# Decay of the RWKV-7 state taken out of the transposed keys: an identity product in place of a POOL product, transposes in place of a diagonal product

## The chip, the core and the metric

The kernel runs on one core of one Trainium2 chip, in one launch. The metric is the device time of that core in microseconds (us), as the median of a few executions; lower is better. The core has a matrix engine (TensorE, PE in the profile, with its weight loads as PEld), a vector engine (VectorE, DVE), an activation engine (ScalarE, ACT), a general engine (GpSimd, POOL) and a queue engine (SyncE, SP). Each works through its own instructions in a fixed order, and semaphores hold an instruction back until what it needs is there. Matrix results land in PSUM, in banks of 512 float32 columns; everything else lies in SBUF.

## What is computed

The reference is a trunk of two layers on a sequence of 512 tokens of 1024 features. Layer 0 mixes tokens with a spatial gating MLP, layer 1 with RWKV-7 time mixing; each is followed by a gated feed-forward block with a causal convolution, and an RMS norm stands ahead of each part and at the end. The change lies in the time mixing alone. Its core, per head (16 heads of 64 features), is a recurrence over tokens on a 64 x 64 state:

```python
def step(state, inp):
    r_t, w_t, k_t, v_t, a_t, b_t = inp
    sa = jnp.einsum('bhvk,bhk->bhv', state, a_t)
    state = (state * w_t[:, :, None, :]
             + sa[..., None] * b_t[:, :, None, :]
             + v_t[..., None] * k_t[:, :, None, :])
    y_t = jnp.einsum('bhvk,bhk->bhv', state, r_t)
    return state, y_t
```

Here w is a decay between 0 and 1 for each feature and token, `exp(-exp(...))` of a low-rank projection; a is minus the normalised key, and b the normalised key times a gate. Behind the recurrence come a group norm, a bonus term r·k·v, an output gate and the projection w_o.

## The kernel before

The work runs in phases: sgu, ffn0, rwkv, ffn1, and the final norm. Dense products are made in three passes of a split float32 (lines 283 to 285: high x high, high x low, low x high). Only the rwkv phase matters here, and in it two loops.

The recurrence is done in chunks of C = 64 tokens, NCH = 8 chunks. With the cumulated decay inside a chunk, the products of all its tokens become small matrix products, and a 64 x 64 triangular system per chunk and head is inverted once. Two heads share the 128 partitions: head 0 the lower half, `H[0]`, head 1 the upper half, `H[1]`. A pair p is two heads; there are 8 pairs, four to a group g.

**The pairs loop** (`pairs`, line 914) walks the pairs. For each, `decay` (line 814) is run two pairs ahead. It makes the cumulated log decay `th`: a tanh on ACT (line 824), plus one on DVE (line 827), a scan along the tokens on DVE (line 829). From it come `gt = exp(C1*th)`, the decay from the chunk's start up to each token; `ei = exp(-C1*th)`, its inverse; and `gc` (line 835), the decay over a whole chunk. It also makes the key's norm, with products on PE (lines 841 and 849). `operands` (line 853), one pair ahead, multiplies: `ar` holds key and receptance times the decay, `bk` holds `b * ei` and `k * ei` (lines 871 and 873), and `rr = rr * kp` for the bonus is made on POOL (line 874). `products` (line 878) makes the chunk's inner products on PE (line 892), masks them on DVE (line 896) and stores them in DRAM (`std`). Then it makes the transposed keys `bt` with the decay to the chunk's end. For that, DVE lays out `dg`, a diagonal matrix of `gc` for each chunk (line 885), PE multiplies `bk` by it (line 907: 16 products for a pair), ACT copies the result and a DMA stores it in DRAM (`btd`).

In `invert` (line 941) the triangular systems of a group are inverted; most of that is a long run of DVE operations (lines 966 and 967) and 32 x 32 products (lines 987 and 990).

**The scan** (`scan`, line 1032) runs group 0, then group 1, over the 8 chunks. In each chunk `st` (inner products), `bt` and `vu` are loaded from DRAM. `vu` holds for each head the state in one half of the partitions and v in the other. A chunk has three steps, each ending in a `yield`. Step A: the product with the state and v into the bank `us` (line 1059), its copy `wt` on DVE (line 1061), the receptance's product into the bank `e` (line 1063), and, on POOL, `s0`, the state times `gc` (line 1068, one instruction a head). Step B: the inverse applied (line 1072, into `us`), and the result copied over the state's place in `vu`, head 0 by DVE (line 1073), head 1 by ACT (line 1074). Step C: the update of the state into `us` (line 1079), the new state as `us + s0` on DVE into the next chunk's `vu` (line 1082, one instruction a head), the rest of the output into `e` (line 1084) and its copy `y` on ACT (line 1087). Every second chunk a `finish` (line 1095) is started, a few instructions per step: group norm (square on ACT, sum on DVE line 1103, power on POOL line 336, product on DVE line 1106), transposes on PE (line 1110), gate and bonus.

**The order of the work.** A scheduler lays out each engine's order beforehand. `weave` (line 1215) runs a main generator and, after each of its steps, pulls `rate` steps (a fraction is carried over) of a fill generator: dense products on PE that fill what the main loop leaves. A pulled step may be placed no earlier than the end of the main step `lag` steps back. `RATES` (line 31) holds rate and lag for five places: two in the pairs loop, then scan 0, scan 1, and the last `finish`. In the pairs loop and scan 0 the fill is `projections` (keys and values); in scan 1 it is `project` (w_o), which for a group pulls 16 dense steps of two k-tiles, six products each, and yields empty until that group's outputs are gated. `scan(1)` has 24 steps; group 0 is gated in its fifth. In `value` (line 783) v is stored to DRAM (`vtd`), from which the scan loads it.

A PSUM accumulator with a tag (`aux`, `e`, `us`, `mm`) is one bank, two to a tag.

Of the kernel before, what the change touches and what calls it, by code (L numbers as in the profile page):

```python
# [24 lines left out]
C = 64  # L25
# [2 lines left out]
GN_EPS = 64e-5  # L28
C1 = -0.5 * math.exp(-0.5)

RATES = ((1.9, 2), (1.9, 6, 2.2), (0.8, 2, 2), (0.75, 2), (2, 2))
WB = 4
FIRST0, WAIT, STEPS = 1, 1, (2, 2, 2, 2, 2)
NKEY = 3
# [15 lines left out]
NG = 2 * 16 + 8  # L50


COFF = dict(ident=0, bones=128, center=256, masks=384, smask=512, causal=1024, blk2=1152, one=1154, id2=1155)
NCST = 1219


def constants():
    c = np.zeros((P, NCST), np.float32)
    i = np.arange(P)
    same = (i[:, None] // C) == (i[None, :] // C)  # L60
    c[:, 0:128] = np.eye(P)
    c[:, 128:256] = same
    c[:, 256:384] = np.eye(P) - same / C
    s, t = (i % C)[:, None], np.arange(C)[None, :]
    c[:, 384:448] = s < t
    c[:, 448:512] = s <= t
    c[:, 512:1024] = (np.arange(T) % C != 0)[None, :]
    c[:, 1024:1152] = i[:, None] <= i[None, :]
    c[:, 1152:1154] = (i[:, None] // C) == np.arange(2)[None, :]
    c[:, 1154] = 1.0  # L70
    c[:, 1155:1219] = (i % C)[:, None] == np.arange(C)[None, :]
    return c


# [68 lines left out]
class Emit:  # L143
# [558 lines left out]
    def rwkv_main(self, r, ctx, gain):  # L702
# [10 lines left out]
        def tile_(shape, tag, bufs):  # L713
            return ep.tile(shape, F32, tag=tag, bufs=bufs, name=self.uid(tag))
# [7 lines left out]
        def bc(t, n):  # L722
            return t.unsqueeze(2).to_broadcast([t.shape[0], t.shape[1], n])
# [17 lines left out]
        def projections():  # L741

            load = Ahead([lambda n=n, m=m: self.parts(n, m, m % 3 == 2) for n in PARTS for m in range(KT)])

            def key(m, a):
                while m >= NKEY and m - NKEY not in used:
                    yield
                ks[m] = tmp("key", NKEY, T)
                S.copy(ks[m], a)

            for m in range(KT - 2):
                a = self.acc("mm")
                yield from self.dense_steps(a, load.take(), r.xk)
                yield from key(m, a)
                yield

            ws = [load.take(), load.take(False)]
            accs = [self.acc("mm") for _ in range(2)]
            xv = []
            for k in range(KT):  # L760
                for j in range(2):
                    self.mm3(accs[j], self.wcols(ws[j], k * P, P), r.xk[k], k == 0, k == KT - 1)
                while len(xv) < min(k + 3, KT):
                    xv.append(r.mix(3, len(xv)))
                if k == 4:
                    load.fetch()
                yield
            for j in range(2):
                yield from key(KT - 2 + j, accs[j])
            late = iter(())  # L770
            for m in range(KT):
                a = self.acc("mm")
                for _ in self.dense_steps(a, load.take(), xv):
                    yield
                    next(late, None)
                for _ in late:
                    yield
                v = ip.tile([P, T], F32, tag="v", bufs=1, name=self.uid("v"))
                S.copy(v, a)
                late = value(m, v)  # L780
            yield from late
# [32 lines left out]
        def decay(p, u):  # L814

            k, w = ks[p], slice(p % 2 * P, (p % 2 + 1) * P)
            accs = [self.acc("e") for _ in range(2)]
            for j in range(2):
                nc.tensor.matmul(accs[j], l2[j][:, w], r.lr[j], start=True, stop=False)
            for j in range(2):  # L820
                nc.tensor.matmul(accs[j], l2[2][H[j], w], r.lr[j][H[j]], start=False, stop=True)
            th, u.ta = scratch("sq"), tmp("ta", 2, T)
            for j, x in enumerate((th, u.ta)):
                S.activation(x, accs[j], AF.Tanh, scale=0.5, bias=dq(j, p))
            u.kn = tmp("kn", 2, T)
            S.activation(u.kn, k, AF.Copy, scale=dq(2, p))
            V.tensor_scalar(th, th, 1.0, None, ALU.add)
            yield
            V.tensor_tensor_scan(th, self.c("smask", T), th, 0.0, ALU.mult, ALU.add)
            sq = scratch("sq")  # L830
            S.activation(sq, u.kn, AF.Square)
            u.gt = tile_([P, NCH, C + 1], "gt", 1)
            G.memset(u.gt[:, :, 0:1], 1.0)
            S.activation(u.gt[:, :, 1:], c3(th), AF.Exp, scale=C1)
            S.activation(gc[:, p], c3(th)[:, :, C - 1], AF.Exp, scale=C1)
            u.ei = scratch("rb")
            S.activation(u.ei, th, AF.Exp, scale=-C1)

            q = self.acc("e")
            for b in range(4):  # L840
                nc.tensor.matmul(q[:, 2 * b:2 * b + 2], sq[:, b * P:(b + 1) * P], self.c("blk2", 2), start=True, stop=True)
            n2 = tile_([P, 8], "n2", 2)
            V.tensor_scalar(n2, q[:, 0:8], 1e-24, None, ALU.max)
            V.reciprocal(n2, n2)
            yield
            u.q = self.acc("e")
            for b in range(4):
                for hd in range(2):
                    nc.tensor.matmul(u.q[H[hd], b * P:(b + 1) * P], n2[:, 2 * b + hd:2 * b + hd + 1].to_broadcast([P, C]),
                                     self.c("ident", P), start=True, stop=True)  # L850
            yield

        def operands(p, u):

            g, i = divmod(p, 4)
            k, rr = ks[p], rt[g][:, i, :]
            gt, ei, kn, ta = u.gt, u.ei, u.kn, u.ta
            kp = scratch("ss")
            S.activation(kp, ta, AF.Identity, scale=dq(4, p), bias=dq(5, p))

            ar = u.ar = tile_([P, NCH, 2 * C], "ar", 2)
            V.tensor_tensor(ar[:, :, 0:C], c3(kn), gt[:, :, 0:C], ALU.mult)
            V.tensor_tensor(ar[:, :, C:], c3(rr), gt[:, :, 1:], ALU.mult)
            for hd in range(2):
                o = 2 * P * hd
                nc.sync.dma_start(std[g][:, H[hd], i, o:o + P].rearrange("c p t -> p c t"), ar[H[hd]])

            bk = u.bk = tile_([P, NCH, 3 * C], "bk", 2)
            V.tensor_tensor(kn, kn, u.q, ALU.mult)
            V.scalar_tensor_tensor(ta, ta, 1.0, ei, ALU.add, ALU.mult)  # L870
            V.scalar_tensor_tensor(bk[:, :, 0:C], c3(kn), -0.5, c3(ta), ALU.mult, ALU.mult)
            V.tensor_tensor(kp, kp, k, ALU.mult)
            V.tensor_tensor(bk[:, :, C:P], c3(kp), c3(ei), ALU.mult)
            G.tensor_tensor(rr, rr, kp, ALU.mult)
            used.add(p)
            S.copy(bk[h1, :, P:], bk[h1, :, 0:C])

        def products(p, u):
# [1 line left out]

            g, i = divmod(p, 4)
            ar, bk = u.ar, u.bk

            dg = tile_([P, NCH, C], "dg", 1)
            V.tensor_tensor(dg, self.c("id2", C).unsqueeze(1).to_broadcast([P, NCH, C]), bc(gc[:, p], C), ALU.mult)
            masks = self.c("masks", P)

            for ch in (slice(0, U), slice(U, NCH)):
# [15 lines left out]
            qs = [self.acc(tag).rearrange("p (c t) -> p c t", t=C) for tag in ("aux", "us")]  # L904
            for c in range(NCH):
                for hd in range(2):
                    nc.tensor.matmul(qs[hd][:, c, :], bk[H[hd], c, C * hd:C * hd + P], dg[H[hd], c, :],
                                     start=True, stop=True)
            for hd in range(2):
                S.copy(bt[:, :, hd, :], qs[hd])  # L910
            nc.sync.dma_start(btd[:, :, p].rearrange("c p a t -> p c (a t)"), bt.rearrange("p c a t -> p c (a t)"))
# [120 lines left out]
        def scan(g, late=iter(())):  # L1032
# [3 lines left out]
            for c in range(NCH):  # L1036
# [20 lines left out]

                for i, hd in ih:
                    nc.tensor.matmul(us[H[hd], 0, i, :], ar(i, hd, 0), vu[:, hd, i, :], start=True, stop=True)  # L1059
                wt = tile_([P, 4, C], "wt", 4)  # L1060
                V.tensor_copy(wt, us[:, 0])
                for i, hd in ih:
                    nc.tensor.matmul(e[H[hd], 0, i, :], ar(i, hd, 1), vu[:, hd, i, :],
                                     start=i == 0, stop=False, skip_group_check=True)
                if not last:
                    s0 = tile_([P, 4, C], "wt", 4)
                    for hd in range(2):
                        G.tensor_tensor(s0[H[hd]], vu[H[hd], hd], bc(gc[H[hd], 4 * g:4 * g + 4, c], C), ALU.mult)
                self.step(late)
                yield  # L1070
                for i, hd in ih:
# [4 lines left out]
                yield  # L1076
                if not last:
                    for i, hd in ih:
                        nc.tensor.matmul(us[H[hd], 0, i, :], bt[:, i, hd, :], vu[:, hd, i, :], start=True, stop=True)
                    nvu = chunks[g, c + 1][2]  # L1080
                    for hd in range(2):
                        V.tensor_tensor(nvu[H[hd], hd], us[H[hd], 0], s0[H[hd]], ALU.add)
                for i, hd in ih:
                    nc.tensor.matmul(e[H[hd], 0, i, :], pt(i, hd), vu[H[hd], hd, i, :],
                                     start=False, stop=True, skip_group_check=True)
# [187 lines left out]
```

## Time and profile before

| | us |
|---|---|
| median of 3 runs | 1321.42 |
| lowest and highest | 1318.86 and 1322.74 |
| profiled execution | 1320.36 |
| its span, first to last instruction | 1318.5 |

In the profiled execution, the pairs loop runs from about 594 to 762 us of the span, scan 0 from 773, scan 1 from about 846 to 906; sgu and ffn0 lie ahead, the rest of `project`, ffn1 and the final norm behind. The profile page gives busy time and number of instructions of each engine, and of each group of instructions by line, with what the engine was waiting for just before them. A view of stretches gives the busy time of each engine in a stretch of time, with the clock that was granted to TensorE (1.00 is full speed). The chain of work is followed back from the last instruction: at each step to whatever released it, or to the instruction before it on its engine. A timeline row has start and length in us, engine, line, what is written from what, the shape and, in brackets, idle time of the engine just before it and who ended it. A float32 product on PE leaves two records (two weight loads and two matmuls), and a matmul's record is longer than the distance from one to the next, because matmuls are pipelined.

### The profile page before, as it was taken

What the parts mean: (1) busy time and instruction counts of PE and PEld (TensorE: products, weight loads), DVE (VectorE), ACT (ScalarE), POOL (GpSimd) and SP (SyncE); (2) the same over time, 40 slices, a digit from 0 to 9 for tenths busy, and PEclk for the clock granted to TensorE, in tenths of its full rate; (3) what the DMA queues carried; (4) which work ended last, traced back from release to release, by engine and by line L of the source; (5) the groups of instructions that cost most, each with busy time, mean ns of one, the idle gap of its engine ahead of it and who ended that gap; (6) DMA issues with size and microseconds to landing.
All of it is one profiled execution on the core that took longest, in us unless ns stands there. A gap on an engine that the chain in (4) does not pass through costs nothing.

```text
span 1318.5 us, 19535 instructions
## 1 busy us (share of the span) xinstructions
PE 1271.9 (96%) x7618; PEld 1027.9 (78%) x7618; DVE 848.0 (64%) x1363; ACT 626.4 (48%) x1064; POOL 141.8 (11%) x152
## 2 busy tenths in 40 slices
PE   8999999999999999999999978898999999999996
PEld 6778888888888888786777757676888888888886
DVE  5565488887775434865879575666687777772223
ACT  5544455555554333565667545333554445442221
POOL 3100200000000100311121011332300000000001
PEclk9999999999999999999999887999999999999998
DMA  7232345555556743245887695971333332233332
GB/s 261 85 112 80 112 148 173 166 168 174 170 174 213 219 141 109 88 126 165 246 254 215 181 237 134 214 190 43 96 96 97 96 96 96 96 92 96 96 89 76
DMA packets 100461, 188.55 MB, mean 143 GB/s; under 512 B 16912, under 2 KB 47760, under 8 KB 100368
## 3 DMA queue, kind: packets, MB, share of 16 engines
q10 hardware_dynamic: 36448, 109.46, 27.2%
q1 hardware_dynamic: 63920, 77.84, 20.7%
q8 instruction: 60, 0.98, 0.3%
q14 instruction: 33, 0.27, 0.1%
HBM read 146.70 MB, written 40.57 MB: 142 GB/s over the span
## 4 chain that ended last, share of the span: by engine, by line
PE 77%; DVE 8%; ACT 3%; DMA 3%; issue 2%; POOL 1%; ACTq 0%; SPq 0%; DVEq 0%; POOLq 0%
PE mm L283 8%; PE mm L284 8%; PE mm L285 8%; PE e L283 5%; PE e L284 5%; PE e L285 5%; PE us L283 5%; PE us L284 5%; PE us L285 5%; PE aux L283 5%; PE aux L284 5%; PE aux L285 5%; PE us L1059 1%; DVE tt L967 1%; DMA vu<-vtd 1%
## 5 line engine op out<-in xcount | busy, mean ns | idle before, releaser
L211 ACT CAST wh<-w 128x512 fp32r<-128x512 f32 (+1 forms) x361 | 220.4, 612 | 399.1 <-PE mm L284 107.0
L212 DVE TENSOR_TENSOR wl<-w,wh 128x512 fp32r<-128x512 f32 x353 | 242.6, 689 | 185.2 <-ACT wh L211 181.2
L283 PE MATMUL mm<-mxh,wh 128*128 128x512 f32 x392 | 161.9, 414 | 1.4 <-ACT mxh L1131 0.8
L285 PE MATMUL mm<-mxh,wl 128*128 128x512 f32 x392 | 155.8, 397 | 0.9 <-DMA wl<-wkd 0.6
L284 PE MATMUL mm<-mxl,wh 128*128 128x512 f32 x392 | 156.1, 398 | 0.3 <-DVE mxl L1132 0.3
L310 POOL TENSOR_TENSOR ss<-ss,sq 128x512 f32<-128x512 f32 x30 | 41.3, 1375 | 777.0 <-issue 594.8
L283 PEld LDWEIGHTS mm<-mxh,wh 128*128 128x128 f32 x392 | 74.8, 191 | 21.0 <-issue 3.6
L506 ACT ACTIVATE cv<-z,par 128x512 f32<-128x512 f32 x88 | 71.7, 817 | 35.9 <-DVE z L504 35.9
L285 PEld LDWEIGHTS mm<-mxh,wl 128*128 128x128 f32 x392 | 74.5, 190 | 17.9 <-DMA wl<-wkd 1.0
L284 PEld LDWEIGHTS mm<-mxl,wh 128*128 128x128 f32 x392 | 74.7, 191 | 16.4 <-DVE mxl L1132 1.2
L283 PE MATMUL e<-mxh,wh 128*128 128x512 f32 x216 | 84.5, 391 | 0.0
L283 PE MATMUL us<-mxh,wh 128*128 128x512 f32 (+1 forms) x216 | 84.4, 391 | 0.0
L285 PE MATMUL us<-mxh,wl 128*128 128x512 f32 (+1 forms) x216 | 84.1, 389 | 0.0
L284 PE MATMUL us<-mxl,wh 128*128 128x512 f32 (+1 forms) x216 | 84.1, 389 | 0.0
L284 PE MATMUL e<-mxl,wh 128*128 128x512 f32 x216 | 84.0, 389 | 0.0
L285 PE MATMUL e<-mxh,wl 128*128 128x512 f32 x216 | 84.0, 389 | 0.0
L507 DVE SCALAR_TENSOR_TENSOR cv<-z,par,cv 128x512 f32<-128x512 f32 x88 | 66.0, 751 | 23.9 <-ACT cv L506 23.9
L283 PE MATMUL aux<-mxh,wh 128*128 128x512 f32 x208 | 81.2, 391 | 0.1
L285 PE MATMUL aux<-mxh,wl 128*128 128x512 f32 x208 | 81.1, 390 | 0.0
L284 PE MATMUL aux<-mxl,wh 128*128 128x512 f32 x208 | 80.9, 389 | 0.0
L508 DVE SCALAR_TENSOR_TENSOR cv<-z,par,cv 128x512 f32<-128x512 f32 x88 | 66.0, 752 | 2.9
L283 PEld LDWEIGHTS e<-mxh,wh 128*128 128x128 f32 x216 | 40.5, 188 | 8.8 <-issue 0.5
(1070 smaller groups left out, 2673.3 us busy)
## 6 DMA issues: line engine op xcount, KB each, us to landing
w<-in_wup ACTq DMA_DIRECT2D x88, 512.0 KB, 3.5
w<-in_wdn ACTq DMA_DIRECT2D x32, 512.0 KB, 3.6
st<-std SPq DMA_DIRECT2D x32, 384.0 KB, 6.0
std<-lq SPq DMA_DIRECT2D x32, 256.0 KB, 4.4
w<-in_wdn ACTq DMA_DIRECT2D x16, 384.0 KB, 3.2
w<-in_wsu ACTq DMA_DIRECT2D x8, 512.0 KB, 3.5
w<-in_wso ACTq DMA_DIRECT2D x8, 512.0 KB, 3.5
pw<-in_wk SPq DMA_DIRECT2D x16, 256.0 KB, 3.9
```

What stands on the lines that cost most here:

```text
L211: nc.scalar.copy(hi[r, :n], src)
L212: (lo_eng or nc.vector).tensor_tensor(lo[r, :n], src, hi[r, :n].bitcast(F32), ALU.subtract)
L283: mm(acc, wh, xh, start=first, stop=False)
L284: mm(acc, wh, xl, start=False, stop=False)
L285: mm(acc, wl, xh, start=False, stop=last)
L310: nc.gpsimd.tensor_tensor(self.ss, self.ss, self.sq, ALU.add)
L506: nc.scalar.activation(c, z[:, 2:], AF.Identity, scale=cw(2, i), bias=self.p("conv_b", l * 44 + i))
L507: nc.vector.scalar_tensor_tensor(c, z[:, 1:T + 1], cw(1, i), c, ALU.mult, ALU.add)
L508: nc.vector.scalar_tensor_tensor(c, z[:, 0:T], cw(0, i), c, ALU.mult, ALU.add)
L967: V.tensor_tensor(tt[:, 0:nj, j + 1:32], tt[:, 0:nj, j + 1:32], q, ALU.add)
L1059: nc.tensor.matmul(us[H[hd], 0, i, :], ar(i, hd, 0), vu[:, hd, i, :], start=True, stop=True)
```

## The change

The keys `bk` are in the frame of the chunk's first token (divided by the decay so far). Before, they were brought to the chunk's end by the diagonal product, and the old state by `s0`; now both are brought there together, after they are summed: state' = gc * (state + bt·[u; v]).

- `products`: `dg` and its DVE operation are gone, with the constant `id2` from which it was made. PE transposes `bk` against the identity.
- `scan`: `s0` on POOL is gone. In chunks 1 to 6, PE adds the state to the sum by a product with the identity, into the second half of the bank `e` (in chunk 0 the state is zero). The update's product is accumulated onto it there, no longer in `us`. DVE then multiplies the sum by `gc`, one instruction a head, in place of the addition. `wt` gets two buffers instead of four, as it shared them with `s0`.
- `decay`: plus one by ACT instead of DVE, behind the two tanh and `kn`.
- `operands`: `rr * kp` by DVE instead of POOL.
- `v` gets two buffers, and the fill's rate in scan 1 is 0.7 instead of 0.75.

```diff
-RATES = ((1.9, 2), (1.9, 6, 2.2), (0.8, 2, 2), (0.75, 2), (2, 2))
+RATES = ((1.9, 2), (1.9, 6, 2.2), (0.8, 2, 2), (0.7, 2), (2, 2))
...
-                v = ip.tile([P, T], F32, tag="v", bufs=1, name=self.uid("v"))
+                v = ip.tile([P, T], F32, tag="v", bufs=2, name=self.uid("v"))
...
-            V.tensor_scalar(th, th, 1.0, None, ALU.add)
+            S.activation(th, th, AF.Identity, bias=self.c("one", 1))
...
-            G.tensor_tensor(rr, rr, kp, ALU.mult)
+            V.tensor_tensor(rr, rr, kp, ALU.mult)
...
-            dg = tile_([P, NCH, C], "dg", 1)
-            V.tensor_tensor(dg, self.c("id2", C).unsqueeze(1).to_broadcast([P, NCH, C]), bc(gc[:, p], C), ALU.mult)
...
-                    nc.tensor.matmul(qs[hd][:, c, :], bk[H[hd], c, C * hd:C * hd + P], dg[H[hd], c, :],
-                                     start=True, stop=True)
+                    nc.tensor.transpose(qs[hd][:, c, :], bk[H[hd], c, C * hd:C * hd + P], self.c("ident", P)[H[hd], H[hd]])
...
-                wt = tile_([P, 4, C], "wt", 4)
+                wt = tile_([P, 4, C], "wt", 2)
...
-                if not last:
-                    s0 = tile_([P, 4, C], "wt", 4)
-                    for hd in range(2):
-                        G.tensor_tensor(s0[H[hd]], vu[H[hd], hd], bc(gc[H[hd], 4 * g:4 * g + 4, c], C), ALU.mult)
+                if 0 < c < NCH - 1:
+                    for i, hd in ih:
+                        nc.tensor.matmul(e[H[hd], 1, i, :], self.c("ident", P)[H[hd], H[hd]], vu[H[hd], hd, i, :],
+                                         start=False, stop=False, skip_group_check=True)
...
                     for i, hd in ih:
-                        nc.tensor.matmul(us[H[hd], 0, i, :], bt[:, i, hd, :], vu[:, hd, i, :], start=True, stop=True)
+                        nc.tensor.matmul(e[H[hd], 1, i, :], bt[:, i, hd, :], vu[:, hd, i, :],
+                                         start=False, stop=True, skip_group_check=True)
...
                     nvu = chunks[g, c + 1][2]
                     for hd in range(2):
-                        V.tensor_tensor(nvu[H[hd], hd], us[H[hd], 0], s0[H[hd]], ALU.add)
+                        V.tensor_tensor(nvu[H[hd], hd], e[H[hd], 1], bc(gc[H[hd], 4 * g:4 * g + 4, c], C), ALU.mult)
```

More of the change, by code (lines that the diff above doesn't have):

```diff
@@ L50 @@
 NG = 2 * 16 + 8
-COFF = dict(ident=0, bones=128, center=256, masks=384, smask=512, causal=1024, blk2=1152, one=1154, id2=1155)
-NCST = 1219
+COFF = dict(ident=0, bones=128, center=256, masks=384, smask=512, causal=1024, blk2=1152, one=1154)
+NCST = 1155
 def constants():
@@ L70, in constants @@
     c[:, 1154] = 1.0
-    c[:, 1155:1219] = (i % C)[:, None] == np.arange(C)[None, :]
     return c
```

## The prediction

> **What bounds the kernel now.** I read the page first (engines, clock), then the busy time by stretches, then the chain of work for each stretch, and last the timeline and the groups by line where the edits lie.
>
> ```profile
> span 1318.5 us, 19535 instructions
> PE 1271.9 (96%) x7618; PEld 1027.9 (78%) x7618; DVE 848.0 (64%) x1363; ACT 626.4 (48%) x1064; POOL 141.8 (11%) x152
> ```
> ```profile
> 594.00:762.00 168.00, 160.38 (x1363) 122.32 (x1362) 120.93 (x216) 108.73 (x204) 22.73 (x22) 0.96 0.73 210
> 700.00:740.00 40.00, 38.65 (x294) 30.00 (x294) 38.69 (x96) 24.23 (x52) 4.98 (x3) 1.00 0.90 259
> 762.00:774.00 12.00, 4.81 (x20) 2.96 (x18) 9.24 (x21) 6.05 (x10) 1.85 (x4) 0.78 0.97 241
> 774.00:836.00 62.00, 56.01 (x835) 43.91 (x834) 40.93 (x96) 29.04 (x60) 12.49 (x14) 0.82 0.76 184
> 836.00:860.00 24.00, 19.36 (x337) 15.89 (x337) 16.23 (x38) 9.19 (x23) 8.38 (x11) 1.00 0.97 217
> 860.00:906.00 46.00, 46.00 (x574) 34.38 (x573) 28.39 (x61) 14.08 (x33) 14.94 (x16) 1.00 0.57 142
> 906.00:911.00 5.00, 1.97 (x10) 1.32 (x9) 2.85 (x4) 0.95 (x2) 2.86 (x2) 1.00 0.00 0
> 911.00:915.00 4.00, 3.92 (x21) 3.56 (x21) 2.31 (x7) 0.71 (x2) 0.00 (x0) 0.64 0.40 135
> ```
> The columns are: stretch, length, then busy us (and instructions) of PE, PEld, DVE, ACT, POOL, then the granted clock, the DMA share and GB/s. As a whole TensorE is the bound, but nothing outside 594 to 915 us is edited (but for a constant table 64 columns narrower). The pairs loop (594 to 762) keeps PE, DVE and ACT all busy and saturates none of them, except that DVE is full from 700 to 740 (38.69 of 40). Then comes a wait at the handover, the first scan (774 to 847, with the second block inversion in it), the second scan, in which PE is full from 860 to 906, and a short hole behind it.
>
> ```profile
> by line: PE mm L283 6.3%; PE mm L285 5.5%; DVE tt L967 5.4%; PE mm L284 5.4%; DVE lq L896 5.2%; DVE pr L966 4.9%; DMA std<-lq 4.2%; issue 4.2%; ACT ix L957 3.7%; PE e L841 3.4%; PE aux L907 3.1%; DMA w<-in_l 2.8%; DMA wl<-wkd 2.7%; ACTq L26
> 625.30 1.70 DVE bk L873
> 667.71 0.60 DVE ss L872
> 669.95 1.78 DVE bk L873
> 692.23 0.61 ACT kn L826
> 718.07 0.60 DVE dg L885
> 735.72 0.60 DVE dg L885
> ```
> This is the chain of the pairs loop (start, us, what). It hops between engines, so an engine's saving counts where the chain is on that engine, and 0.3% of the time (4 us) is about what a measurement can tell from no change.
>
> **Pairs loop.** The groups by line of the edited work and its neighbours (busy us, mean ns):
> ```profile
> L873 DVE TENSOR_TENSOR bk<-ss,rb 128x512 f32<-128x512 f32 x8 | 9.8, 1220 | 0.0
> L885 DVE TENSOR_TENSOR dg<-cst,gc 128x512 f32<-128x512 f32 x8 | 6.4, 804 | 1.7 <-PE us L907 1.7
> L872 DVE TENSOR_TENSOR ss<-ss,key 128x512 f32<-128x512 f32 x8 | 5.5, 684 | 2.8 <-ACT ss L859 2.8
> L827 DVE TENSOR_SCALAR sq<-sq 128x512 f32<-128x512 f32 x8 | 3.4, 420 | 4.8 <-ACT sq L824 4.8
> L826 ACT ACTIVATE kn<-key,dpar 128x512 f32<-128x512 f32 x8 | 5.8, 719 | 0.1
> L874 POOL TENSOR_TENSOR rt<-rt,ss 128x512 f32<-128x512 f32 x8 | 14.2, 1770 | 50.5 <-DVE ss L872 39.6 <-DVE ar L863 10.9
> ```
> DVE loses dg (8 x 0.80 = 6.4 us) and the add of one (8 x 0.42 = 3.4). It gains rr (8 x 0.68, the price of L872, which has the same shape, = 5.5). It also loses a collision: L873 has the same form as L872 and takes 1.22 against 0.68, since the POOL product L874 becomes ready with it, at the end of L872. That excess, 8 x 0.54 = 4.3, goes with POOL's product. In full DVE is freed of 6.4 + 3.4 - 5.5 + 4.3 = 8.6 us. ACT gains the add, priced as L826: 8 x 0.72 = 5.8. It now stands behind ta and kn on ACT's queue, so the scan of a unit can start later by these; that unit's products come a whole pair later, and this slack hides it. If it does not, ACT's share is paid in full.
>
> ```profile
> 630.52 0.32 PE L907 MATMUL aux<-dg,bk 64*128 64x64 f32 x1
> ...
> 632.45 1.09 PE L849 MATMUL e<-cst,n 128*64 128x128 f32 x16
> ```
> ```profile
> L907 PE MATMUL aux<-dg,bk x128: 215/272/392, 630.5 to 759.5; 64*128 64x64 f32 x128
> L907 PE MATMUL us<-dg,bk x128: 213/272/398, 630.5 to 759.5; 64*128 64x64 f32 x128
> ...
> L1110 PE MATMUL aux<-cst,y x32: 272/273/476, 812.1 to 911.2; 128*128 128x128 f32 x32
> ```
> On PE, L907 (its first record and what follows its last) takes 632.45 - 630.52 = 1.9 us a pair. Its 128 matmuls leave 256 records, two each, whereas the 32 transposes of L1110 (8 calls of four) leave 32, one each. So the transposes should take half: 0.95 us a pair, 7.7 in all.
>
> What of this is on the chain: L907 has 3.1% of 168 us = 5.2, half of it goes: -2.6. The two contended L873 that are shown stand 1.1 over the 0.60 of ss L872, and a third contention like them is in the pieces between (L871 beside POOL, my estimate from these two): -3.3. The two dg: -1.2. rr adds 0.6 wherever ss L872 is on the chain, by my count four pairs in the whole of this chain: +2.4. The add on ACT adds 0.7 where kn is on it, by my count twice: +1.4. Sum -3.3. That is the cautious end, because between 700 and 740 DVE works without a break and there every DVE edit counts, also those that the chain passes by. The other end is DVE in full, -8.6. I take the middle, **-6.0**. Each number bears errors of the new static order of instructions on top, which no row prices; the ends are widened by PE's 2.6 below and to 0 above. The wait at the handover (762 to 774) is a store and a reload of v through DRAM and stays; v's second buffer only lets a copy start early: 0. Of the wt buffers half were s0's, so half serve as before: 0.
>
> **Scans.** POOL's product s0 goes and costs nothing today except by contention; the identity product comes.
>
> ```profile
> 840.25 0.68 PE L1084 MATMUL e<-vu,st 64*64 64x64 f32 x14
> 840.42 0.88 DVE L1082 TENSOR_TENSOR vu<-us,wt 64x256 f32<-64x256 f32 x2 [0.36 <-PE us L1079]
> ```
> ```profile
> 861.95 0.39 PE L284 MATMUL mm<-mxl,wh 128*128 128x512 f32 x1
> 862.18 0.40 PE L285 MATMUL mm<-mxh,wl 128*128 128x512 f32 x1
> 862.50 0.68 PE L1072 MATMUL us<-wt,ti 64*64 64x64 f32 x16
> 863.12 0.50 PE L284 MATMUL mm<-mxl,wh 128*128 128x512 f32 x1
> ```
> The identity product has the shape of L1072: 863.12 - 862.50 = 0.6 us for its 16 records, in chunks 1 to 6 of each scan, 12 times. In 860 to 906 PE is full, and five of them fall there: +3.1. In 774 to 836 five more lie in a stretch where PE sits idle 6 of 62 us and the inversion holds it up: 0, at most +3.1. Two fall in 836 to 860.
>
> The new DVE product reads the bank e, into which L1084 writes afterwards. Today L1082 reads the bank us and L1084 runs beside it (840.25 and 840.42).
> ```profile
> ACT vu L1074 <- DVE vu L1073: 22.9, 9, 4.6
> ```
> These two copies read disjoint halves of one bank, and ACT waits for DVE nine times: the program lets no two engines into one bank together. So I expect L1084 to wait for both new products, 841.30 - 840.25 = 1.05 us, with the next chunk's L1059 behind it on PE. [...]
>
> Where projection steps are at hand, they fill that 1.05 us: 0 in 860 to 906 and 774 to 836. In 836 to 860 no fill is left, so L1084's 0.6 comes ahead of L1059 three times, +1.8, and two identity products, +1.2.
> ```profile
> by line: POOL gr L336 13.7%; DVE y L1106 9.2%; PE us L1072 8.4%; PE us L1059 7.0%; PE aux L1110 5.5%; DVE gs L1103 5.4%; PE mm L283 5.0%; issue 5.0%; DVE vu L1073 4.9%; DVE rt L1113 3.7%; DVE wt L1061 3.6%; PE e L1084 2.8%; PE aux L283 2.8%
> 841.87 1.09 DVE L1106 TENSOR_TENSOR y<-y,gr 128x512 f32<-128x512 f32 x1 [0.58 <-POOL gr L336]
> 881.68 0.69 DVE L1106 TENSOR_TENSOR y<-y,gr 128x512 f32<-128x512 f32 x1
> ```
> But the chain there runs through the normalisation (gs, gr, y), which hides part of such PE work: I count half of 3.0, +1.5. L1106 takes 1.09 beside s0 and 0.69 without, twice on this chain: -0.8. Together **+0.7**, ends -0.8 and +3.0.
>
> The rate: scan 1 gives 24 steps; 24 x 0.75 = 18 pulls, 3 of them before group 0 is gated and empty; 24 x 0.7 gives 16, 2 empty. So 14 steps instead of 15 run inside. A step is six matmuls of 0.23 (862.18 - 861.95), 1.4 us, and moves into the hole at 906 to 911, where PE is busy 1.97 of 5: 860 to 906 gets +3.1 - 1.4 = **+1.7**. Behind the hole the clock is 0.64 over 4 us; with the hole halved I take it to stay up, 0.36 x 4 = **-1.4**, ends -1.4 and 0.
>
> **Sum:** -6.0 + 0.7 + 1.7 - 1.4 = -5.0. The profiled execution took 1320.36 us (span 1318.5 and 1.86 around it), 1.06 below the median 1321.42 of the runs; the change is set against the median: 1316.4.
>
> **Rivals.** (1) No measurable change, 1319.8: the pairs loop is tied to its order and to the DRAM handover, DVE's relief ends in a wait for the fill, and only PE's -2.6 is left of the -6.0. For it: DVE is the chain in one stretch of 40 us alone. Against: the contended L873 are on the chain. A change that doesn't do what it says belongs here too: if the transposes take two passes each, -2.6 is lost, 1319.0. (2) Slower, 1329.5: the fill is not placed between L1079 and L1084, and PE stands 1.05 us in each of the 11 other chunks with a following chunk (+11.6), and the normalisation hides nothing (+1.5 more). It decides from the ninth bare wait on, since 9 x 1.05 takes the gain of 5.0 and the 4 that a measurement can tell. For it: the fill's place is fixed beforehand. Against: today fill stands before L1079 and after L1084 alike (L284 at 863.12 right behind L1072).
> (3) Slower still, by the clock:
> ```profile
> 745.00:750.00 5.00, 5.00 (x71) 3.45 (x70) 1.24 (x2) 4.88 (x9) 0.00 (x0) 0.50 0.43 106
> 845.00:855.00 10.00, 8.47 (x158) 7.17 (x159) 5.61 (x15) 3.10 (x8) 3.17 (x3) 1.00 1.02 226
> ```
> If each pair's transposes brought the 0.50 of the first row for 5 us, PE would lose 2.5 us eight times: 1336. [...] In the second row a group of L1110 transposes runs and the clock is 1.00 throughout, so the trace speaks against it for bursts this short.
>
> **How the numbers follow.** Forecast 0.45, rival 1 0.35, rival 2 0.17, rival 3 0.03: faster by over 0.3% 0.45, within it 0.35, slower 0.20. The low end is pairs -11.2, scans -0.8 and +1.7, hole -1.4: -11.7, and about 2 us for the order, 1308; the high end reaches into rival 2, 1327.
>
> **What would show it.** Right: L873 near 0.68, L907 with 128 records and about 0.95 us a pair, no dg, pairs loop 4 to 9 us shorter, vu at 1082 a read of e at 0.42 with L1084 starting behind it among fill matmuls, 860 to 906 longer by 1 to 3 us, hole below 2 us at full clock. Wrong: PE idle before L1084 with DVE as releaser in most chunks; a pairs loop of the same length; a clock below 0.9 where the transposes run.

## The result and the profile after the change

The change makes the kernel slower. After it the median is 1329.42 us (1324.49 to 1331.38), against 1320.64 us (1318.86 to 1322.74) for the kernel before beside it; the ratio is 1.0061 with a 95% interval of 1.0044 to 1.0078, or +8 us, where -5 was forecast. The profiled execution after took 1329.71 us, its span 1327.9.

The head of its page, and its busy time by the stretches that were shown of before (stretch, length, busy us and instructions of PE, PEld, DVE, ACT, POOL, then granted clock, DMA share and GB/s):

```profile
span 1327.9 us, 19587 instructions
...
PE 1271.5 (96%) x7682; PEld 1028.5 (77%) x7682; DVE 835.3 (63%) x1355; ACT 629.7 (47%) x1072; POOL 109.3 (8%) x116
```
```profile
594.00:762.00 168.00, 158.55 (x1249) 120.79 (x1248) 113.02 (x209) 114.07 (x215) 8.76 (x14) 0.94 0.72 210
762.00:774.00 12.00, 0.00 (x0) 0.00 (x0) 9.02 (x23) 4.72 (x7) 0.61 (x2) 0.58 0.99 230
774.00:836.00 62.00, 55.79 (x902) 43.46 (x902) 38.23 (x91) 28.14 (x57) 5.86 (x4) 0.89 0.75 181
836.00:860.00 24.00, 18.68 (x358) 16.13 (x360) 12.54 (x32) 6.29 (x17) 3.88 (x4) 0.93 0.95 213
860.00:906.00 46.00, 44.56 (x585) 33.49 (x581) 25.28 (x58) 14.32 (x34) 7.32 (x5) 0.96 0.56 140
```

In the pairs loop DVE works 7.9 us less, near the 8.6 that the sum gave, and PE 1.8 us less; ACT works 5.3 us more, near the add's 5.8. What has changed for the worse is the clock (0.94 where it was 0.96, 0.93 and 0.96 where it was 1.00; from 774 to 836 it is better, 0.89 for 0.82) and PE's idle time: it is no longer full from 860 to 906, and it does nothing from 762 to 774. So I looked for waits.

To see where, I cut both spans at three instructions: the first product of the second block inversion (DVE; it starts when the pairs loop has delivered), the copy wt of chunk 0 of scan 1, and the last copy y of scan 1. Timeline rows of the kernel before, of the kernel after, and of experiment e5, which will be told below:

```profile
767.03 0.62 DVE L966 TENSOR_TENSOR pr<-li,tt 128x31 f32<-128x31 f32 x1
...
847.08 0.42 DVE L1061 COPY wt<-us 128x256 f32<-128x256 f32 x1 [1.91 <-PE us L1059]
...
904.92 0.74 ACT L1087 COPY y<-e 64x256 f32<-64x256 f32 x2 [0.23 <-PE e L1084]
```
```profile
766.09 0.19 DVE L961 TENSOR_TENSOR pr<-li,tt 128x31 f32<-128x31 f32 x1
...
848.66 0.43 DVE L1056 COPY wt<-us 128x256 f32<-128x256 f32 x1 [1.91 <-PE us L1054]
...
913.38 0.75 ACT L1084 COPY y<-e 64x256 f32<-64x256 f32 x2 [0.23 <-PE e L1081]
```
```profile
760.07 0.19 DVE L961 TENSOR_TENSOR pr<-li,tt 128x31 f32<-128x31 f32 x1
...
840.48 0.42 DVE L1056 COPY wt<-us 128x256 f32<-128x256 f32 x1 [1.91 <-PE us L1054]
...
900.20 0.74 ACT L1086 COPY y<-e 64x256 f32<-64x256 f32 x2 [0.23 <-PE e L1083]
```

| us | before | after | e5 | forecast |
|---|---|---|---|---|
| up to the inversion (pairs loop) | 767.0 | 766.1 (-0.9) | 760.1 (-7.0) | -6.0 |
| inversion to scan 1 | 80.1 | 82.6 (+2.5) | 80.4 (+0.4) | 0, and +0.7 from 836 to 860 |
| scan 1 | 57.8 | 64.7 (+6.9) | 59.7 (+1.9) | +1.7 |
| behind scan 1 | 413.6 | 414.5 (+0.9) | 413.6 (0) | -1.4 |
| span | 1318.5 | 1327.9 (+9.4) | 1313.8 (-4.7) | -5.0 |

Two places carry it: the pairs loop's gain did not arrive, and scan 1 takes 6.9 us longer. Each column is one execution; the three took 1320.36, 1329.71 and 1315.60 us, within 0.3 us of the medians 1320.64, 1329.42 and 1315.54.

**Pairs loop.** The groups of the edited lines after (L872 is bk, L873 rr, L903 the transposes, L826 the add of one, L828 the scan of the decay, L842 the key norm; busy us, mean ns, idle before and its releaser):

```profile
L828 DVE TENSOR_TENSOR_SCAN sq<-cst,sq 128x512 f32<-128x512 f32 x8 | 9.8, 1219 | 11.6 <-ACT sq L826 11.6
L903 PE MATMUL aux<-cst,bk 64*128 64x64 f32 x64 | 6.9, 243 | 0.0
L903 PE MATMUL us<-cst,bk 64*128 64x64 f32 x64 | 6.8, 240 | 0.0
L872 DVE TENSOR_TENSOR bk<-ss,rb 128x512 f32<-128x512 f32 x8 | 6.5, 808 | 0.0
L826 ACT ACTIVATE sq<-sq,cst 128x512 f32<-128x512 f32 x8 | 5.8, 720 | 0.1
L873 DVE TENSOR_TENSOR rt<-rt,ss 128x512 f32<-128x512 f32 x8 | 5.5, 683 | 0.0
L842 DVE TENSOR_SCALAR n<-e 128x8 f32<-128x8 f32 x8 | 1.3, 159 | 9.2 <-PE e L840 9.2
```

The prices are nearly as forecast: the transposes leave 128 records in place of 256, rr costs 0.68, the add on ACT 0.72; bk fell from 1.22 to 0.81 us, not all the way to 0.68. But DVE now stands 11.6 us in front of the scan of the decay, where it stood 4.8 us in front of the add before (5.4 of the 11.6 lie at the very first pair), and 9.2 us in front of the key norm, where it stood 6.2. It spends what it was given on waiting.

**Scan 1.** Chunk 1, from the timeline after (start, us):

```profile
859.55 0.69 PE L1074 MATMUL e<-vu,cbt 128*64 128x64 f32 x16
859.66 0.69 DVE L1125 TENSOR_TENSOR rt<-rt,aux 128x512 f32<-128x512 f32 x1 [0.27 <-PE aux L1123]
...
861.68 0.50 PE L282 MATMUL mm<-mxh,wh 128*128 128x512 f32 x1 [1.44 <-ACT mxh L1128]
861.69 1.43 DVE L1129 TENSOR_TENSOR mxl<-rt,mxh 128x256 fp32r<-128x256 f32 x4
...
863.04 0.87 DVE L1079 TENSOR_TENSOR vu<-e,gc 64x256 f32<-64x256 f32 x2
...
865.36 1.06 PE L1081 MATMUL e<-vu,st 64*64 64x64 f32 x16
```

The update L1074 is done at 860.2. Its product on DVE, L1079, stands behind the gating work (L1125 to L1129) in DVE's queue, starts at 863.0 and ends at 863.9, and only behind it does L1081 write into the other half of bank e. Behind the fill that PE has in its order by then, L1081 starts at 865.4, over 5 us behind the update, not 1.05. Fill does stand between them, as the prediction said, but it waits for ACT (mxh) itself, so PE is first bare for 1.44 us; and the clock, in this chunk and the one before it, does this:

```profile
850.00:852.00 2.00, 1.01 (x16) 0.73 (x16) 1.52 (x5) 0.37 (x1) 0.83 (x1) 1.00 1.03 236
852.00:854.00 2.00, 1.56 (x27) 1.45 (x29) 1.07 (x2) 0.48 (x2) 0.80 (x1) 0.65 1.01 200
854.00:856.00 2.00, 2.00 (x39) 1.88 (x37) 0.42 (x1) 0.25 (x1) 0.00 (x0) 0.50 1.10 274
860.00:862.00 2.00, 0.56 (x10) 0.28 (x5) 1.94 (x4) 1.95 (x6) 0.00 (x0) 1.00 0.12 34
862.00:864.00 2.00, 2.00 (x7) 1.46 (x7) 1.88 (x6) 0.55 (x2) 0.00 (x0) 0.71 0.55 135
864.00:866.00 2.00, 2.00 (x16) 1.26 (x16) 0.00 (x0) 0.00 (x0) 0.00 (x0) 0.50 0.33 127
```

Twice, behind 2 us in which PE was busy for half or a quarter, the clock is at 0.50 for some 3.4 us (from about 852.6 to 856.0 and from 862.8 to 866.2, in stretches of half a us; 0.35 x 2 + 0.50 x 2 = 1.7 us of full clock lost the first time, 0.29 x 2 + 0.50 x 2 = 1.6 the second). That is up to 3.3 of the 6.9 us, an estimate from the clock alone, since from 852 to 854 PE was not full either.

### The profile page after: what moved, and what is told of

It reads as the page before. It is cut to its first block, busy times and chain, and to the rows that moved or that the text cites. A ratio compares the mean times of both kernels' runs of the same rounds, so it can differ in the third digit from the quotient of the medians.

```text
span 1327.9 us, 19587 instructions
## 1 busy us (share of the span) xinstructions
PE 1271.5 (96%) x7682; PEld 1028.5 (77%) x7682; DVE 835.3 (63%) x1355; ACT 629.7 (47%) x1072; POOL 109.3 (8%) x116
## 4 chain that ended last, share of the span: by engine, by line
PE 81%; DVE 6%; ACT 3%; DMA 2%; issue 2%; POOL 1%; ACTq 0%; DVEq 0%; POOLq 0%
PE mm L282 9%; PE mm L283 8%; PE mm L284 8%; PE e L282 5%; PE e L283 5%; PE e L284 5%; PE us L282 5%; PE us L284 5%; PE us L283 5%; PE aux L282 5%; PE aux L284 5%; PE aux L283 5%; PE us L1054 1%; DMA vu<-vtd 1%; PE e L1081 1%
```

## The experiments

The theories: (1) the new state's sum shares bank e with the output, so that L1081 waits for DVE, and PE's stops cost standing time and clock; (2) the add of one on ACT takes back DVE's gain in the pairs loop. The rivals: the identity products' own time on PE; the handover through DRAM, where PE stands 14.7 us instead of 7.1; POOL's relief; the fill's rate. Medians are in us; every ratio is to the kernel before on the same chip, and 0.001 of it is 1.3 us.

| run | edit | median | before | ratio, 95% interval |
|---|---|---|---|---|
| (the change) | | 1329.42 | 1320.64 | 1.0061 [1.0044, 1.0078] |
| e1_own_bank | sum in a bank of its own | 1321.97 | 1321.51 | 1.0000 [0.9983, 1.0017] |
| e2_add_on_dve | add of one back on DVE | 1320.32 | 1321.51 | 0.9988 [0.9966, 1.0009] |
| e3_rr_on_pool | rr back on POOL | 1328.77 | 1321.51 | 1.0055 [1.0035, 1.0076] |
| e4_rate_75 | rate back at 0.75 | 1329.74 | 1321.51 | 1.0069 [1.0044, 1.0095] |
| e5_bank_and_add | e1 and e2 together | 1315.54 | 1320.80 | 0.9962 [0.9943, 0.9981] |
| e6_both_rr_pool | e5, rr on POOL | 1321.92 | 1320.80 | 1.0015 [0.9995, 1.0035] |
| e7_no_identity | e5 without identity product | 1313.01 | 1320.80 | 0.9944 [0.9924, 0.9963] |
| e8_pt_first | changed kernel, L1081 ahead of L1079 | 1322.49 | 1320.80 | 1.0028 [1.0008, 1.0048] |
| e9_add_behind_th | e1, add on ACT right behind its tanh | 1321.00 | 1322.11 | 0.9992 [0.9980, 1.0004] |
| e10_vu_first | e5, vu loaded ahead of st | 1311.80 | 1322.11 | 0.9929 [0.9909, 0.9950] |
| e11_before_add_act | before, only the add on ACT | 1321.13 | 1322.11 | 0.9987 [0.9967, 1.0008] |
| e12_before_rr_dve | before, only rr on DVE | 1321.60 | 1322.11 | 0.9996 [0.9982, 1.0011] |
| e13_both_vu_late | as e5 | 1317.61 | 1321.30 | 0.9968 [0.9945, 0.9990] |
| e14_both_vu_first | as e10 | 1314.84 | 1321.30 | 0.9952 [0.9934, 0.9970] |
| e15_after_vu_first | changed kernel, vu first | 1327.54 | 1321.30 | 1.0048 [1.0029, 1.0067] |
| e16_vu_first_rate_75 | e14, rate 0.75 | 1311.69 | 1321.30 | 0.9926 [0.9900, 0.9952] |

**The bank: e1 and e8.**

```diff
+                if not last:
+                    s1 = self.acc("us").rearrange("p (a i f) -> p a i f", a=2, i=4)
-                        nc.tensor.matmul(e[H[hd], 1, i, :], self.c("ident", P)[H[hd], H[hd]], vu[H[hd], hd, i, :],
-                                         start=False, stop=False, skip_group_check=True)
+                        nc.tensor.matmul(s1[H[hd], 0, i, :], self.c("ident", P)[H[hd], H[hd]], vu[H[hd], hd, i, :],
+                                         start=i == 0, stop=False, skip_group_check=True)
```
and likewise the update and the product with `gc` on `s1`.

> The sum of the state goes into a bank of its own (the second of the tag us) in place of the second half of e; the identity product stays, so the bank wait of L1081 (pt) behind the two products on DVE goes, and nothing else. Theory 1 (the scans lose their time to that wait: pt, the y copies and the next chunk's first product stand behind DVE, and the stops bring the clock down): scan 1 6 to 7 us shorter, its last y copy at about 907 instead of 913.4 of the span, the whole 1329.4 -> 1322 to 1325. Rival A (the identity products themselves, 12 times 0.6 us on a full PE, are the price): the whole within 2 us of 1329.4, though pt no longer waits.

In e8 the bank stays shared, and the lines of `nvu` (L1077 to L1079) stand behind the product L1081.

> The kernel after the change with one step moved: the two products of the new state (DVE, reading the second half of e) are emitted behind the last output product L1081 (pt, writing the first half of e) and no longer ahead of it. The bank stays shared. Theory 1 (pt waits for DVE only because both touch one bank): pt runs right behind the update, the new state comes 0.6 us later in each chunk, the y copies on ACT now wait for DVE instead; scan 1 shorter by 3 to 6 us, the whole 1323 to 1326.5. Rival (the wait is hidden by the fill and e1 won by a better order of instructions): within 1.5 us of 1329.4.

e1 takes back 0.0061 of the ratio, 8.1 us, and e8, by a change of order alone, 0.0033 (4.4 us; its interval and that of the changed kernel overlap a little). The same three cuts place it: scan 1 takes 59.7 us in e1 and 60.4 in e8, against 64.7, and the stretch ahead of it 80.1 and 82.3, against 82.6. Chunk 1 in e1:

```profile
853.20 0.69 PE L1076 MATMUL us<-vu,cbt 128*64 128x64 f32 x16
...
853.82 0.68 PE L1083 MATMUL e<-vu,st 64*64 64x64 f32 x16
...
855.33 0.73 PE L282 MATMUL mm<-mxh,wh 128*128 128x512 f32 x2 [0.83 <-ACT mxh L1130]
...
856.70 0.87 DVE L1081 TENSOR_TENSOR vu<-us,gc 64x256 f32<-64x256 f32 x2
```

The output product (L1083 here) follows the update at once, though DVE's product is still 2.9 us away. Whole scan 1, from chunk 0's first product to behind the last output product, in the kernel before, the kernel after, e1, e8 and e7, in this order:

```profile
846.00:905.00 59.00, 56.93 (x767) 43.49 (x762) 37.88 (x83) 20.15 (x47) 18.30 (x19) 1.00 0.68 163
```
```profile
847.50:913.50 66.00, 62.83 (x865) 48.52 (x862) 35.92 (x83) 20.20 (x47) 10.97 (x7) 0.95 0.61 149
```
```profile
843.00:904.00 61.00, 59.44 (x864) 46.60 (x860) 35.72 (x83) 19.89 (x47) 10.37 (x7) 1.00 0.70 160
```
```profile
845.50:907.00 61.50, 59.37 (x861) 46.19 (x857) 35.82 (x83) 19.97 (x47) 11.00 (x7) 1.00 0.65 158
```
```profile
840.50:899.50 59.00, 57.23 (x763) 43.88 (x760) 36.25 (x83) 20.25 (x48) 10.36 (x7) 1.00 0.75 168
```

Without the wait the scan takes 61 us at full clock, 5 less than after the change; 0.05 x 66 = 3.3 of these are clock. Theory 1 holds. The stretch from the inversion to scan 1 gives another 2.5 (82.6 to 80.1), so that by the cuts 7.5 of e1's 8.1 us lie in the two scans. L1081 and L1079 touch different columns of the same partitions of bank e, and the measured remedy is another bank (8.1 us).

**The identity product: e7.** The loop over `c` in 1 to 6 with the identity is left out, so each chunk's sum lacks the state carried over.

> As e5_bank_and_add, but the identity product is left out, so that the state of a chunk is not carried into the next sum: a part of the computation is missing. It prices the identity products: by the prediction's sum 5 of 0.6 us on a full PE in 860 to 906 and two in 836 to 860 with half hidden, 3.1 + 0.6 us less than e5, 0 in scan 0. If they cost their PE time everywhere: 12 x 0.6 = 7.2 us less. If PE has room for them: within 1 us of e5.

The ratio falls by 0.0018, 2.4 us, with overlapping intervals; in the rows above scan 1 goes from 61 to 59 us. That is within the forecast's 3.1 and 0.6, and below the 7.2 of the rival. The product itself is cheap.

**The add of one and rr: e2, e3, e5, e6, e9, e11, e12.**

```diff
-            S.activation(th, th, AF.Identity, bias=self.c("one", 1))
+            V.tensor_scalar(th, th, 1.0, None, ALU.add)
```

> The add of one goes back to DVE, the rest stays changed. Theory 2 (behind ta and kn on ACT it holds the scan of the decay, 11.6 us of DVE idle before it against 4.8, and what DVE gained in the pairs loop is spent there): pairs loop 2 to 4 us shorter, the whole 1325 to 1327.5. Rival B (the pair-long slack hides it, and the handover's wait through DRAM takes whatever the loop gains): the loop ends 0 to 3 us earlier but the first scan product stays at about 776 of the span, the whole 1328 to 1331.

> The bonus product rr goes back to POOL, the rest stays changed. If the contention of POOL and DVE was worth what the prediction took for it (L872 0.68 -> 1.22 us, eight times, less eight rr of 0.68 on DVE: -1.2 net, and 4.3 - 5.5 = -1.2 in the sum of DVE), the whole is within 2 us of 1329.4 and L872 is back near 1.2. Theory 3 (the first scan product is tied to the transfers of the handover, not to DVE): the first scan product stays within 1 us of 776, whatever the loop does.

> Both mends together: the sum of the state in a bank of its own, the add of one on DVE. If the two losses are separate places (e1_own_bank -7.5 us in the scans, e2_add_on_dve -9.1 in the pairs loop, each against 1329.4), they add up: 1311 to 1315, against 1320.6 to 1321.5 of the kernel before, ratio 0.992 to 0.996. Rival (a shared floor, such as the 36 us of the second inversion on DVE or the transfers of the handover, holds the start of scan 1): only one of the two counts, 1318 to 1321.

> As e5_bank_and_add, and the bonus product rr back on POOL. With the add on DVE again, DVE carries the pairs loop and no longer waits for ACT, so the contention of POOL's product with L872 (1.22 or 1.49 us instead of 0.68) now counts; against it DVE loses rr, 0.68 a pair. By the sum of DVE -1.2 us or so in favour of DVE: within 2 us of e5. If the contention sits on the chain more often than rr does, e6 is 2 to 4 us longer than e5; if rr is on the chain more often, 2 to 4 shorter.

> The kernel before, with one part of the change alone: the add of one on ACT, behind ta and kn. By the prediction's sum it costs nothing and frees DVE of 3.4 us: -3 to 0. By the theory of the add holding the scan: the pairs loop loses as much as after the change, +2 to +9, less what DVE was late anyway for its contended L873 (rr on POOL in e3 and e6 was free when the add was on ACT): 1320.6 -> 1322 to 1328.

> The kernel before, with one part of the change alone: rr on DVE. By the prediction's terms -4.3 of contention and +5.5 of rr: +1.2 in the sum of DVE, or -0.9 on its chain. By e6 against e5 (rr on DVE won 6.4 us there): 1314 to 1317. L873 back at 0.68.

e9 is e1 with the add moved up:

```diff
             for j, x in enumerate((th, u.ta)):
                 S.activation(x, accs[j], AF.Tanh, scale=0.5, bias=dq(j, p))
+                if j == 0:
+                    S.activation(th, th, AF.Identity, bias=self.c("one", 1))
...
-            S.activation(th, th, AF.Identity, bias=self.c("one", 1))
```

> The state's sum in a bank of its own, as e1_own_bank; the add of one stays on ACT but stands directly behind the tanh of th, ahead of the tanh of ta and of kn. If the place on ACT's queue is what held the scan of the decay (ta and kn ahead of it, 0.7 us each, and whatever ACT does between), most of what e2 won comes back and DVE is spared its 3.4 us too: 1312 to 1317, DVE idle before the scan on ACT under 4 us. If it is ACT itself (any third ACT step between tanh and scan costs, as ACT is busy), 1318 to 1322, close to e1.

e2 gains 0.0073 (9.6 us), more than I had expected, and e5 0.0038 over e1 (5.0 us): theory 2 holds in the changed kernel. The two mends lie in different places: together they gain 0.0099 (13.1 us), less than 8.1 + 9.6 = 17.7, but no more so than their intervals allow. The waits of DVE in the pairs loop, in e2, in e11 and in e9 (engine, what, released by: us, times, longest):

```profile
DVE n L842 <- PE e L840: 3.8, 3, 3.1
...
DVE sq L826 <- ACT sq L823: 2.9, 3, 2.0
```
```profile
DVE sq L829 <- ACT sq L827: 6.5, 2, 5.6
DVE n L843 <- PE e L841: 5.8, 5, 3.7
```
```profile
DVE n L843 <- PE e L841: 12.2, 6, 4.3
DVE sq L829 <- ACT sq L825: 9.1, 5, 5.8
```

In the old kernel (e11) the same add on ACT costs nothing: but for the first pair (5.6 us) DVE waits there 0.9 us. Its contended bk (1.45 us there) probably keeps it late; no run takes that alone away from e11. In the changed kernel, where DVE has less to do, it arrives early: 11.6 us of waiting in front of the scan and 9.2 in front of the key norm, where e2 has 2.9 and 3.8. The other profiles agree: with the add on ACT behind kn and rr on DVE (e1, e4, e8, e15) 10.4 to 12.3 and 7.7 to 9.1, with both on DVE (e5, e7, e10, e13, e14, e16) 2.9 to 4.2 and 3.8 to 7.2. So the cost comes about only when the other edits work. But my picture of why was too simple: I put it down to ta and kn ahead on ACT's queue, and e9, where the add goes ahead of them, gains nothing clear over e1 (0.9992 against 1.0000). The wait in front of the key norm is even longer there, 12.2 us. The add's place also changes the order of PE: by the records of the traces, the key norm's products of the last three pairs stand behind 146, 176 and 206 of the products L888 in e1, and behind 128, 166 and 192 in e5. Whether ACT's 0.72 us a pair or this order is what costs, no run here separates.

rr behaves likewise. Alone on DVE it is worth nothing in the old kernel (e12) and nothing where the add is on ACT (e3), but 0.0053 (7.0 us) where the add is on DVE (e6 against e5). There POOL's product stretches bk further than in the old kernel, to 1.63 us, shown by e6's row:

```profile
L872 DVE TENSOR_TENSOR bk<-ss,rb 128x512 f32<-128x512 f32 x8 | 13.0, 1628 | 0.0
```

So in these runs moving rr pays only where the diagonal product is gone and the add stays on DVE. That each edit alone only moves the loop's limit elsewhere is how I read the waits; the removal of the diagonal product was not run by itself.

**Handover and rate: e4, e10, e13 to e16.**

```diff
+            for hd in range(2):
+                nc.sync.dma_start(vu[H[1 - hd], hd], vtd[c, H[1 - hd], ps])
+                if c == 0:
+                    G.memset(vu[H[hd], hd], 0.0)
             for hd in range(2):
                 o = P * (1 - hd)
                 nc.sync.dma_start(st[H[hd], o:o + 12 * P], std[g][c, H[hd]].rearrange("p i t -> p (i t)"))
-            for hd in range(2):
-                nc.sync.dma_start(vu[H[1 - hd], hd], vtd[c, H[1 - hd], ps])
-                if c == 0:
-                    G.memset(vu[H[hd], hd], 0.0)
```

> As e5_bank_and_add, with v and the state's place loaded ahead of the inner products in each chunk's load. Theory (the wait of the first scan product for vu at the handover, 12.9 us of idle PE in e5, lies beside the second block inversion on DVE, which starts by itself at 760 and ends 37 us later): the first scan product starts 2 us or more earlier, scan 1 no earlier, the whole within 1.5 us of e5. Rival (the wait for vu is the bound there): the whole 2 to 5 us less than e5.

> The kernel of e5_bank_and_add again, as the base on this chip for the next runs: 1313 to 1318, ratio to the kernel before 0.994 to 0.998.

> The kernel of e10_vu_first again, beside its base. If the wait for vu at the handover binds, 2 to 5 us less than e13 and scan 0 starts as much earlier; if it lies beside the second inversion, within 1.5 us of e13.

> The kernel after the change, with nothing mended but the order of the loads: v and the state's place ahead of the inner products. If the doubled wait at the handover (7.1 -> 14.7 us) took part of the gain of the pairs loop: 1324 to 1327. If it lies beside the inversion, which starts at 766.1 in any case: 1328 to 1331.

After the change PE waits twice as long for vu at the handover, before and after:

```profile
PE us L1059 <- DMA vu<-vtd: 7.1, 1, 7.1
```
```profile
PE us L1054 <- DMA vu<-vtd: 14.7, 1, 14.7
```

Loading vu first lowers the ratio three times: e10 under e5 by 0.0033, e14 under e13 by 0.0016, e15 under the change by 0.0013, each time with overlapping intervals. None is clear by itself; taken together, weighted by their intervals, they make some 0.0020 (0.0004 to 0.0036), about 2.6 us. Most of the 7.6 us by which PE's wait grew is therefore not lost: the inversion runs beside it on DVE (it started at 766.1 while PE stood until 776.2), and scan 1 needs what it delivers.

> The rate of the fill in scan 1 goes back to 0.75, the rest stays changed. Theory 4 (the lower rate moves a fill step of 1.4 us to behind the last chunk, where it should have filled the hole; the hole stayed 3.1 us all the same): scan 1 is 1 to 1.5 us longer, the tail as much shorter, the whole within 1.5 us of 1329.4. If the lower rate starved PE in scan 1 and let its clock fall there (0.57 at 852 to 856), the clock of 860 to 906 rises over 0.98 and the whole falls by 2 us or more.

> As e14_both_vu_first, with the rate of the fill in scan 1 back at 0.75. By the prediction one step of six matmuls (1.4 us) moves from the hole behind the last chunk into the scan, where PE is full: 0 to +1.5 us, and the hole one step emptier. If PE has room in the scan: -1.5 to 0.

The rate makes no difference in the changed kernel (1.0069 against 1.0061). In the mended one 0.75 is lower by 0.0026, again with overlapping intervals, and the profiles do not lay that to the rate: scan 1, where it acts, takes 60.2 us in e16 and 60.0 in e14, while the pairs loop, which it does not touch, ends at 755.6 and 761.7. e16 has the lowest median of all: 1311.69 us, 0.7% under the kernel before, without anything that the change does being given up but the place of an add, of a sum, of a load and the old rate.

## Why the prediction was wrong

**Where it failed.** Two steps. First: "Where projection steps are at hand, they fill that 1.05 us: 0 in 860 to 906 and 774 to 836." The wait for the bank was seen, and that fill would stand there too. But the wait was priced at the duration of the two DVE products, not at the time until DVE gets to them: in chunk 1 of scan 1 they stand behind the gating work, and L1081 came 5 us late. And the fill left PE idle for 0.99 of 2 us and for 1.44 of 2 us, and behind both the clock was at 0.50. e1 puts this step at 8.1 us, of which 5.0 are seen in scan 1 and 2.5 ahead of it. Second: the add on ACT, of which it said that the "unit's products come a whole pair later, and this slack hides it. If it does not, ACT's share is paid in full." It does not, and what is paid is not ACT's 5.8 us of work but the gain of the edits beside it: 5.0 (e5 against e1) to 9.6 us (e2 against the change).

**What was right.** The prices of single operations (rr 0.68, add 0.72, transposes one record each; the contention of bk is gone, 0.68 us, once the add is back on DVE, while 0.13 of its 0.54 us stays after the change). The pairs loop's -6.0, once the add is back on DVE: -7.0 in e5's profile. A profile of the same kernel as e13 has only -1.0; its execution took 1321.8 us, 4 above its median, where e5's lay at its median. The identity products and the rate in 860 to 906, +1.7: scan 1 is 1.9 longer in e5 than before. With both steps mended the whole comes out as forecast: 0.9962 and 0.9968 of 1321.4 are 1316.4 and 1317.2, against 1316.4. That it meets so closely is in part luck, since the loop gave 1.0 more in e5 and the hole 1.4 less than the sum had. DVE's sum for rr alone, +1.2 by busy time or -0.9 on its chain, agrees with e12's nothing.

**What else missed.** The hole behind scan 1 was to shrink by a step and keep its clock (-1.4). It did not:

```profile
914.00:919.00 5.00, 2.31 (x11) 1.53 (x9) 2.38 (x4) 1.37 (x3) 2.86 (x2) 1.00 0.00 0
919.00:926.00 7.00, 6.08 (x26) 4.89 (x27) 4.61 (x12) 1.42 (x4) 0.20 (x4) 0.63 0.24 75
```

PE is busy 2.31 of 5 us, where it was 1.97: the fill stood right behind the last output product, and the hole begins when it is used up. The clock behind it is 0.63 over 7 us, where it was 0.64 over 4; from 926 to 930 it is still 0.79, while before it was back at 1.00 seven us behind the hole. In e5, with the same fill, the 4 us behind the hole have 0.70.

**The rivals.** Rival 2 gave 1329.5, and 1329.4 was measured; that the two agree is luck, for only half of it came by its mechanism. L1081's wait for DVE is real, as it said, yet it is paid in a few chunks by clock and by DVE's queue, not by 1.05 us eleven times: the view of waits has L1081 (its weight loads) waiting for L1079 six times in both scans, 3.2 us in all. The other half is the lost gain of the pairs loop, which is rival 1. I had let the two exclude each other, while they lie in different places and add up: -5.0 + 8.1 + 5.0 is +8. Rival 3 (transposes pull the clock down) is refuted: e16 has the same transposes and from 594 to 742 a clock of 1.00.

```profile
594.00:656.00 62.00, 59.16 (x406) 43.74 (x406) 41.40 (x70) 39.11 (x74) 3.00 (x6) 1.00 0.75 217
656.00:742.00 86.00, 82.60 (x683) 61.80 (x680) 73.33 (x146) 60.61 (x116) 4.40 (x6) 1.00 0.84 248
```

## What to carry to other kernels

Price a new wait by when the engine that is waited for will reach its instruction in its own queue, not by how long that instruction takes (5 us against 1.05 in chunk 1 here); and where one engine reads an accumulator while another writes, try them in different banks, which was worth 8.1 us here (e1). An operation moved off a busy engine may be free only as long as that engine stays late: the add on ACT cost nothing in the kernel before (0.9987, e11), and 5.0 us (e5 against e1) once the other edits had relieved DVE. Where several steps are uncertain in different places, their losses add, and the range should hold the case in which two go wrong.

## What the runs showed of the hardware

The clock fell behind stops of PE shorter than I had looked for: PE was idle for 0.99 of 2 us ahead of one low stretch and for 1.44 ahead of the other, and I had looked for stops of the length of the hole (3 us). But such a stop does not always bring it. In the kernel before, PE was idle for 1.00 of the 2 us shown here, and the clock stayed at 1.00 then and from there to 906:

```profile
844.00:846.00 2.00, 1.00 (x24) 0.72 (x21) 1.17 (x5) 0.37 (x1) 0.00 (x0) 1.00 0.95 200
```

So these runs give no length of stop from which the clock falls.

The pairs loop varies by itself. The same kernel, run as e5 and as e13, has it at clock 0.96 and 0.93:

```profile
594.00:762.00 168.00, 154.85 (x1248) 115.61 (x1246) 120.31 (x226) 112.16 (x209) 9.09 (x16) 0.96 0.77 221
```
```profile
594.00:762.00 168.00, 161.79 (x1253) 120.96 (x1251) 116.50 (x217) 110.60 (x208) 8.72 (x14) 0.93 0.75 214
```

The second inversion starts at 760.1 in the one and at 766.0 in the other, and the spans are 1313.8 and 1320.0. So a difference of 5 us in this loop between two single profiles says little; the -7.0 above leans on e5's profile, and the verdicts on the add and on rr rest on the ratios.

Read together, the profiles are more regular than one by one: the loop ends earlier the higher its clock (594 to 755 us). With add and rr on DVE it ends at 755.6 and 756.6 for a clock of 1.00 (e16, e2), at 760.1 for 0.97 (e5), at 760.6 to 761.7 for 0.96 (e7, e10, e14) and at 766.0 for 0.93 (e13). With the add on ACT it ends at 763.8 to 764.2 for 0.96 (e1, e8, e15) and at 766.1 and 767.3 for 0.94 (the change, e4); the kernel before ended at 767.0 for 0.96. So at a clock of 0.96 the edits gain some 3 us in the loop with the add on ACT, and some 6 with it on DVE; this is an estimate from single profiles. Whether waits lower the clock there or the clock makes the waits, the profiles do not show.

What a POOL product beside it costs a DVE product is not one number: the contended bk took 1.22 us in the kernel before, 1.45 in e11, 1.49 in e3 and 1.63 in e6, against 0.68 alone (e5).
